# The last expert's first product before the other's second one, and half of the closing norm on the tensor engine

## The chip, the core and the metric

The kernel runs on one core of a Trainium2 chip. The core has a tensor engine (PE, whose weight loads the profile lists apart as PEld), a vector engine (DVE), a scalar engine (ACT), GpSimd (POOL) and SyncE (SP), which here issues nearly all transfers. Sixteen DMA engines move data between HBM and the on-chip memory (SBUF); PE writes its products to PSUM, eight banks of 128 partitions by 512 float32. The metric is the device time of one execution in microseconds (us).

## What is computed

One layer of a decoder trunk for 256 tokens of width 1024 in float32: a mixer, a norm, a mixture of experts, and a norm again. Only the last two matter here:

```python
def layer_norm(x, g, b):
    mu = jnp.mean(xf, axis=-1, keepdims=True)
    var = jnp.mean(jnp.square(xf - mu), axis=-1, keepdims=True)
    return ((xf - mu) * lax.rsqrt(var + LN_EPS) * g + b)
...
    def expert_block(args):
        h = xblk @ w1[e] + b1[e]                  # 1024 -> 2048
        gate, upv = jnp.split(h, 2, axis=-1)
        gate = jnp.minimum(gate, SWIGLU_LIMIT)
        upv = jnp.clip(upv, -SWIGLU_LIMIT, SWIGLU_LIMIT)
        act = (upv + 1.0) * (gate * jax.nn.sigmoid(SWIGLU_ALPHA * gate))
        return act @ w2[e] + b2[e]                # 1024 -> 1024
...
        h = moe_ffn(x, ...)                       # each token: 4 of 32 experts
        x = layer_norm(ALPHA * x + h, ln2_g[l], ln2_b[l])
```

An expert has 8 MB of w1 and 4 MB of w2; all 32 are read whole, 384 MB.

## The kernel before

The experts run one after the other, 0 to 31 (`E` is 32), each on up to 64 gathered tokens (a branch behind the end, not taken with these inputs, does the rest). Per expert:

- **First product** (`gemm1`, in `Last.first` for expert 31): the tokens stand still in PE 64 columns wide, w1 streams past; two halves (gate and up) fill the upper and lower 64 partitions of two PSUM banks, `h0` and `h1`. ACT and DVE copy the banks to `hs`.
- **Activation** (`act_steps`): PE transposes `hs` in two groups of four, DVE adds the bias, clips and multiplies, ACT takes the sigmoid. The result is `a`.
- **Second product** (`gemm2`, in `Last.second` for expert 31): `a` stands still, w2 streams past; ACT copies the bank to `ys`.
- **Scatter** (`scatter`): four products with the gate weights (`gT`) add `ys` to the four sums `acc[t][h]` (token tile t, column half h) that stay in PSUM.

The weights come in 2 MB loads (16 KB in a row for each partition) into a ring of 11 buffers: four loads for w1, two for w2. All are issued by SP in the order of the code (`in_order`, L1132). Up to expert 29 the order is w1 of expert e, then w2 of expert e-1, so that each second product stands behind the first product of the next expert and its activation is hidden. Behind that it is: w1 of 30, w2 of 30, w1 of 31, w2 of 31. The fourth load of w1 of 31 is cut into four pieces and the two loads of w2 of 31 into four by rows (`Last.load`, L1144). The code between L1358 and L1402 follows that order: second product of 30 (L1360), first product of 31 with the scatter of 30 between its rows, activation of 31 in two halves between the last products (L1371 to L1378), second product of 31. Its rows j 6 and 7 are split into two column halves of 256 (`columns`, L1392).

Calls through `PE`, `DVE` and `ACT` (class `Pinned`) keep the order of the code on their engine; calls through `nc.` may be placed by the scheduler.

The end: `add_sums` takes the moments of each 256 columns of `acc` on DVE (8 times `bn_stats`), `statistics` (L121) combines them and takes the square root on ACT, and `normed` (L1407) writes (x - mean) * rstd * g2 + b2 in four pieces of 128 tokens by 512 columns, each stored on its own. Three pieces are two DVE instructions each; the piece (0, 1) is one ACT instruction and two POOL instructions. `g2` and `b2` are the scale and the bias, spread over all partitions (`norm_rows`, some 110 us before the end).

## Time and profile before

| | |
|---|---|
| median of 3 runs | 1191.1 us (1190.51 to 1191.97) |
| the profiled execution | 1191.24 us |
| its span, first to last instruction | 1189.4 us |
| PE busy | 1126.8 us, 95% |
| DVE, ACT, POOL busy | 347.9, 208.8, 64.1 us |
| HBM traffic | 448 MB, 377 GB/s over the span |

The page of the profile gives busy time of each engine, the span in 40 equal slices, and the chain of waits that ended last. A time in a row is in us from the span's start; a float32 product shows as two matmul records, so that "x8" stands for four products. A bracket such as [0.69 <-ACT t L1212] is idle time of the engine just before the row and what ended it. A busy PE can be a PE that is also kept busy at just the pace of the loads.

### The profile page before, as it was taken

The page shows a single profiled execution, that of the slowest core. Times are in us where ns is not written, and L with a number is a line of the kernel's source. Part 1 is how long each engine was busy: PE and PEld are TensorE (multiplying, and loading weights), DVE is VectorE, ACT ScalarE, POOL GpSimd, SP SyncE. Part 2 cuts the span into 40 slices and gives each one's busy share as a digit, 9 for nine tenths or more (in the row PEclk, how much of TensorE's full clock was granted, in tenths as well). Part 3 has the DMA queues.
Part 4 walks back from the last instruction along what each step waited for, and adds up shares of the span by engine and source line. Part 5 has one row for each costly group of instructions (what it writes and reads, how often), then busy time and mean ns, then how long its engine had stood idle before and what let it go on. Part 6 is the DMA issues. An engine that isn't in the chain of part 4 may idle for free.

```text
span 1189.4 us, 15191 instructions
## 1 busy us (share of the span) xinstructions
PE 1126.8 (95%) x6440; PEld 594.2 (50%) x6441; DVE 347.9 (29%) x713; ACT 208.8 (18%) x494; POOL 64.1 (5%) x106
## 2 busy tenths in 40 slices
PE   9999999999999999999999898989898989899995
PEld 8998889985434343343434242424242424244432
DVE  6679776473111111111111111111111111111114
ACT  5115544432101010101101010101010101011101
POOL 1010001311000000000000000000000000000000
PEclk9999999999999999999999999999999999999998
DMA  8994329779999999999999999999999999999994
GB/s 246 321 298 142 107 75 377 301 272 370 422 430 430 428 430 427 428 429 429 428 428 431 429 430 429 428 428 430 429 429 430 428 429 429 428 429 430 428 417 182
DMA packets 72274, 449.33 MB, mean 378 GB/s; under 512 B 8084, under 2 KB 40778, under 8 KB 47498
## 3 DMA queue, kind: packets, MB, share of 16 engines
q1 hardware_dynamic: 71694, 447.50, 91.8%
q8 instruction: 52, 0.85, 0.3%
q10 hardware_dynamic: 508, 0.81, 0.2%
q14 instruction: 20, 0.16, 0.0%
HBM read 447.25 MB, written 1.05 MB: 377 GB/s over the span
## 4 chain that ended last, share of the span: by engine, by line
DMA 52%; PE 45%; DVE 2%; ACT 0%; issue 0%; SPq 0%; POOL 0%; POOLq 0%; DVEq 0%
DMA w<-in_moe_w_dram 50%; PE h L48 15%; PE u L48 8%; PE mm L94 4%; PE mm L95 4%; PE mm L96 4%; PE acc L48 2%; DMA w<-in_w_in_dram 1%; PE sc L648 1%; PE mm L48 1%; PE yps L693 1%; PE ptp L684 1%; PE sc L48 1%; PE ptp L48 0%; DVE t L48 0%; PE ptp L94 0%
## 5 line engine op out<-in xcount | busy, mean ns | idle before, releaser
L48 PE MATMUL h<-w,t 128*64 128x512 f32 x1448 | 320.1, 593 | 30.0 <-DMA w<-in_moe_w_dram 26.9
L48 PEld LDWEIGHTS h<-w,t 128*64 128x64 f32 x1448 | 101.9, 137 | 237.7 <-issue 181.8
L48 PE MATMUL u<-w,t 128*64 128x512 f32 x960 | 213.3, 596 | 1.5 <-DMA w<-in_moe_w_dram 1.3
L1107 DVE COPY t<-h 128x512 f32<-128x512 f32 x31 | 21.4, 692 | 507.2 <-PE h L48 507.2
L48 PE MATMUL h<-w,rws 128*64 128x512 f32 x640 | 141.6, 595 | 12.9 <-DMA w<-in_moe_w_dram 12.1
L48 PEld LDWEIGHTS u<-w,t 128*64 128x64 f32 x960 | 66.4, 137 | 125.5 <-issue 118.6
L48 PEld LDWEIGHTS h<-w,rws 128*64 128x64 f32 x640 | 44.8, 137 | 104.8 <-issue 81.6
L94 PE MATMUL mm<-xhl,ws 128*128 128x256 f32 x336 | 96.8, 288 | 0.0
L95 PE MATMUL mm<-xhl,ws 128*128 128x256 f32 x336 | 95.0, 283 | 0.0
L96 PE MATMUL mm<-xhl,ws 128*128 128x256 f32 x336 | 94.9, 283 | 0.0
L1106 ACT COPY t<-h 128x512 f32<-128x512 f32 x31 | 18.2, 586 | 434.4 <-PE h L48 434.4
L89 DVE TENSOR_TENSOR ws<-w,ws 128x1024 fp32r<-128x1024 f32 (+1 forms) x64 | 73.3, 1150 | 11.8 <-ACT ws L88 11.0
L1082 POOL TENSOR_TENSOR ext<-ext,G 128x128 f32<-128x128 f32 x62 | 27.1, 456 | 811.8 <-PE h L48 793.1
L48 PE MATMUL acc<-t,ext 64*128 64x512 f32 (+1 forms) x264 | 64.3, 603 | 0.9 <-ACT t L1212 0.7
L94 PEld LDWEIGHTS mm<-xhl,ws 128*128 128x128 f32 x336 | 64.3, 191 | 1.0 <-issue 0.8
L95 PEld LDWEIGHTS mm<-xhl,ws 128*128 128x128 f32 x336 | 64.4, 192 | 0.0
L96 PEld LDWEIGHTS mm<-xhl,ws 128*128 128x128 f32 x336 | 64.3, 191 | 0.0
L1199 DVE SCALAR_TENSOR_TENSOR t<-t 128x512 f32<-128x512 f32 x29 | 20.1, 692 | 150.1 <-PE u L48 150.0
L1212 ACT COPY t<-u 128x512 f32<-128x512 f32 x31 | 18.2, 586 | 177.4 <-PE u L48 177.4
L48 PEld LDWEIGHTS acc<-t,ext 64*128 64x128 f32 x264 | 23.2, 186 | 40.2 <-issue 28.5
L1195 ACT ACTIVATE t<-t 128x512 f32<-128x512 f32 (+2 forms) x36 | 20.7, 582 | 89.8 <-DVE t L1194 84.7
L88 DVE CAST ws<-w 128x1024 fp32r<-128x1024 f32 (+1 forms) x47 | 29.5, 636 | 24.0 <-PE mm L96 15.6
(340 smaller groups left out, 1095.3 us busy)
## 6 DMA issues: line engine op xcount, KB each, us to landing
w<-in_moe_w_dram SPq DMA_DIRECT2D x189, 2048.0 KB
w<-in_w_in_dram SPq DMA_DIRECT2D x22, 1024.0 KB
w<-in_w_up_dram SPq DMA_DIRECT2D x6, 1024.0 KB
w<-in_cmp_w_dram SPq DMA_DIRECT2D x4, 1024.0 KB
w<-in_w_o_dram SPq DMA_DIRECT2D x4, 1024.0 KB
w<-in_moe_w_dram SPq DMA_DIRECT2D x4, 1024.0 KB
w<-in_w_in_dram SPq DMA_DIRECT2D x6, 512.0 KB
w<-in_moe_w_dram SPq DMA_DIRECT2D x4, 512.0 KB
```

The lines of the kernel that those rows point to most:

```text
L48: return lambda *a, **k: self.tc.keep_in_program_order(f(*a, **k))
L88: copy(hi, src)
L89: return sub.tensor_tensor(lo, src, hi.bitcast(F32), op=OP.subtract).ins
L94: pe.matmul(p, ah, bh, start=first, stop=False, **kw)
L95: pe.matmul(p, ah, bl, start=False, stop=False, **kw)
L96: pe.matmul(p, al, bh, start=False, stop=last, **kw)
L1082: nc.gpsimd.tensor_tensor(SG[:, t], S[:, t, x:x + 1].to_broadcast([128, 2, SLOTS]), gsrc[:, t].unsqueeze(2).to_broadcast([128, 2, SLOTS]), ...
L1106: nc.scalar.copy(hs[:, :512], hp[0])
L1107: nc.vector.tensor_copy(hs[:, 512:], hp[1])
L1195: nc.scalar.activation(sg[i], gate[i], AF.Sigmoid, scale=1.702)
L1199: vec.scalar_tensor_tensor(a[:, js], up[i], 1.0, sg[i], op0=OP.add, op1=OP.mult)
L1212: nc.scalar.copy(ys, yp)
```

## The change

Three things are changed, all behind expert 30's activation:

1. **Order.** The loads become w1 of 30, w1 of 31, w2 of 30, w2 of 31. PE runs the whole first product of 31 (now by `gemm1`), the transposes of its activation, the second product of 30, the scatter of 30, and then the second product of 31. The activation of 31 writes to another buffer (`a_last`). Only the last load is cut: 1 MB by rows (j 4 and 5), then two pieces of 0.5 MB by columns, with 1 KB in a row.
2. **The end of the last product.** Column half 0 of rows 6 and 7, its copy, its four scatter products and its moments stand ahead of column half 1.
3. **The norm.** PE adds the bias `b2` through the identity into two free PSUM banks (`biased`, two products of 128x512, ahead of the second product of 31). For token tile 1 DVE makes only (x - mean) * g2, builds a diagonal matrix of rstd, and PE multiplies by it on top of the bias; ACT copies the bank out and issues the store. Token tile 0 is two DVE instructions for each half. POOL has no part in it any more.

```diff
     class Last:
         def load(self):
-            self.w1 = [new_rows(2) for _ in range(4)]
-            for q in range(3):
-                in_order(self.w1[q], w1v[E - 1, q])
-            for c in range(2):
-                for h in range(2):
-                    cs = slice(h * FF + c * 512, h * FF + (c + 1) * 512)
-                    in_order(self.w1[3][:, :, cs], w1v[E - 1, 3, :, :, cs])
             self.w2 = [new_rows(4) for _ in range(2)]
-            for q in range(2):
-                for r in (slice(0, 2), slice(2, 4)):
-                    in_order(self.w2[q][:, r], w2v[E - 1, q, :, r])
+            in_order(self.w2[0], w2v[E - 1, 0])
+            in_order(self.w2[1][:, :2], w2v[E - 1, 1, :, :2])
+            for c in range(2):
+                w, src = [v.rearrange("p r (h c) -> p r h c", h=2)[:, 2:, :, c * 256:(c + 1) * 256]
+                          for v in (self.w2[1], w2v[E - 1, 1])]
+                in_order(w, src)
             return self
...
+    def biased():
+        banks = [u_tile(), h_tile(1)]
+        for h, p in enumerate(banks):
+            PE.matmul(p, ident, b2[:, h * 512:(h + 1) * 512], start=True, stop=False, skip_group_check=True)
+        return banks
...
-            w2 = Second(e).load()
-            last = Last().load()
-            gemm2(a, w2)
...
-    banks = [h_tile(c) for c in range(2)]
-    for k in range(6):
-        for c in range(2):
-            last.first(banks, k, c)
-        if k == 1:
-            scatter(prev[1])
-    last.first(banks, 6, 0)
-    last.first(banks, 7, 0)
-    nc.scalar.copy(hs[:, :512], banks[0])
-    last.first(banks, 6, 1)
-    act(b1T[:, :, E - 1], a_main, 0, DVE, parts=2)
-    last.first(banks, 7, 1)
-    nc.scalar.copy(hs[:, 512:], banks[1])
-    act(b1T[:, :, E - 1], a_main, 1, DVE, parts=2)
+    w1, w2, last = First(E - 1).load(), Second(E - 2).load(), Last().load()
+    gemm1(xg[(E - 1) % 3], w1)
+    steps = [act_steps(b1T[:, :, E - 1], a_last, c, DVE, banks=[b]) for c, b in enumerate((u_tile(), h_tile(1)))]
+    for c in range(2):
+        next(steps[c])
+    gemm2(prev[0], w2)
+    for c in range(2):
+        for _ in steps[c]:
+            pass
+    scatter(prev[1])
+    banks = biased()
     yp = h_tile(0)
     for j in range(6):
         last.second(yp, j, slice(0, 512))
...
-    def normed(st):
+    def normed(st, banks):
         stats = [statistics(st[t]) for t in range(2)]
...
+        for c, p in zip(cols, acc[1]):
+            DVE.scalar_tensor_tensor(y[:, 1, c], p, stats[1][0], g2[:, c], op0=OP.subtract, op1=OP.mult)
+        DVE.reciprocal(stats[1][1], stats[1][1])
+        DVE.tensor_scalar(diag, ident, stats[1][1], None, op0=OP.mult)
+        DVE.reciprocal(stats[0][1], stats[0][1])
+        for c, p in zip(cols, banks):
+            PE.matmul(p, diag, y[:, 1, c], start=False, stop=True, skip_group_check=True)
+            ACT.copy(y[:, 1, c], p)
+            stores.append(nc.scalar.dma_start(ov[:, 1, c], y[:, 1, c]).ins)
+        for c, p in zip(cols, acc[0]):
+            d = y[:, 0, c]
+            DVE.scalar_tensor_tensor(d, p, stats[0][0], g2[:, c], op0=OP.subtract, op1=OP.mult)
+            DVE.scalar_tensor_tensor(d, d, stats[0][1], b2[:, c], op0=OP.mult, op1=OP.add)
+            stores.append(nc.sync.dma_start(ov[:, 0, c], d).ins)
```

How this moves instructions is shown at three places. First PE from the end of expert 31's first product to the split of its second one, before (`h_6716` and `h_6717` hold the first product of 31, `u<-ident` are transposes, `h_6788` is the second product of 31):

```order
L48 MATMUL h_6716<-w,t_3247 64x512 x4
L48 MATMUL h_6717<-w,t_3247 64x512 x2
L48 MATMUL u<-ident,t_3248 128x128 x4
L48 MATMUL h_6717<-w,t_3247 64x512 x2
L48 MATMUL u<-ident,t_3248 128x128 x4
L48 MATMUL h_6788<-w,t_3247 64x512 x12
L48 MATMUL h_6788<-w,t_3247 64x256 x8
```

and the same stretch in the changed kernel (`h_6696` is the first product's second bank, `u<-w` the second product of 30, the four `acc` its scatter, the `gb` rows the bias, `h_6779` the second product of 31):

```order
L48 MATMUL h_6696<-w,t_3247 64x512 x2
L48 MATMUL u<-ident,t_3248 128x128 x4
L48 MATMUL h_6732<-ident,t_3248 128x128 x4
L48 MATMUL u<-w,t_3247 64x512 x16
L48 MATMUL acc_3258<-t_3247,ext 128x512
L48 MATMUL acc_3259<-t_3247,ext 128x512
L48 MATMUL acc_3441<-t_3247,ext 128x512
L48 MATMUL acc_3442<-t_3247,ext 128x512
L48 MATMUL u<-gb_6428,ident 128x512
L48 MATMUL h_6776<-gb_6428,ident 128x512
L48 MATMUL h_6779<-w,rws 64x512 x12
L48 MATMUL h_6779<-w,rws 64x256 x4
```

Between the last first product and the last second product there now stand expert 30's second product, its scatter and the two bias products.

Second, the end of PE's list in the changed kernel, which before was the eight 64x256 products followed by eight `acc` products and nothing more:

```order
L48 MATMUL h_6779<-w,rws 64x256 x4
L48 MATMUL acc_3258<-t_3247,ext 128x256
L48 MATMUL acc_3259<-t_3247,ext 128x256
L48 MATMUL acc_3441<-t_3247,ext 128x256
L48 MATMUL acc_3442<-t_3247,ext 128x256
L48 MATMUL u<-t_3248,ext 128x512
L48 MATMUL h_6776<-t_3248,ext 128x512
```

Column half 1 now stands behind the scatter of half 0, and two products with the diagonal matrix (`ext`) close the list.

Third, DVE behind the moments, before:

```order
L48 BN_AGGR bn_mv<-st_6802 128x2
L48 SCALAR_TENSOR_TENSOR t_3248<-acc_3258,bn_mv,gb_6428 128x512
L48 RECIPROCAL rstd<-rstd 128x1 x2
L48 SCALAR_TENSOR_TENSOR nm<-bn_mv,rstd 128x1
L48 SCALAR_TENSOR_TENSOR t_3248<-t_3248,rstd,gb_6428 128x512
L48 SCALAR_TENSOR_TENSOR t_3248<-acc_3441,bn_mv,gb_6428 128x512
L48 SCALAR_TENSOR_TENSOR t_3248<-t_3248,rstd,gb_6428 128x512
L48 SCALAR_TENSOR_TENSOR t_3248<-acc_3442,bn_mv,gb_6428 128x512
L48 SCALAR_TENSOR_TENSOR t_3248<-t_3248,rstd,gb_6428 128x512
```

and in the changed kernel (`acc_3441` and `acc_3442` are token tile 1):

```order
L48 BN_AGGR bn_mv<-st_6793 128x2
L48 SCALAR_TENSOR_TENSOR t_3248<-acc_3441,bn_mv,gb_6428 128x512
L48 SCALAR_TENSOR_TENSOR t_3248<-acc_3442,bn_mv,gb_6428 128x512
L48 RECIPROCAL rstd<-rstd 128x1
L48 TENSOR_SCALAR ext<-ident,rstd 128x128
L48 RECIPROCAL rstd<-rstd 128x1
L48 SCALAR_TENSOR_TENSOR t_3248<-acc_3258,bn_mv,gb_6428 128x512
L48 SCALAR_TENSOR_TENSOR t_3248<-t_3248,rstd,gb_6428 128x512
L48 SCALAR_TENSOR_TENSOR t_3248<-acc_3259,bn_mv,gb_6428 128x512
L48 SCALAR_TENSOR_TENSOR t_3248<-t_3248,rstd,gb_6428 128x512
```

DVE has six instructions of 128x512 in both; the diagonal matrix comes behind the first two of them, and PE and ACT finish that tile.

## Rows read from the trace of the kernel before

**Rows 1.** The page: span, busy time of the engines, and what the transfers moved in each of 40 slices.

```profile
span 1189.4 us, 15191 instructions
PE 1126.8 (95%) x6440; PEld 594.2 (50%) x6441; DVE 347.9 (29%) x713; ACT 208.8 (18%) x494; POOL 64.1 (5%) x106
GB/s 246 321 298 142 107 75 377 301 272 370 422 430 430 428 430 427 428 429 429 428 428 431 429 430 429 428 428 430 429 429 430 428 429 429 428 429 430 428 417 182
```

**Rows 2.** The chain of waits that ended last, from 1115 us on: start, length, what.

```profile
1119.05 38.99 DMA w<-in_moe_w_dram
1158.06 15.11 DMA w<-in_moe_w_dram
1173.17 0.14 issue
1173.31 1.10 PE h L48 x8
...
1176.62 2.73 DVE st L1389 x8
...
1183.97 0.98 DVE t L48
```

**Rows 3.** Busy time by stretch at the end of the loads: stretch, its length, busy us and instructions of PE, PEld, DVE, ACT, POOL, granted clock of TensorE, busy share of the DMA engines, GB/s.

```profile
1164.00:1166.00 2.00, 2.00 (x11) 0.76 (x8) 0.73 (x2) 0.09 (x1) 0.00 (x0) 1.00 1.04 438
1170.00:1171.00 1.00, 1.00 (x8) 0.47 (x6) 0.66 (x3) 0.00 (x0) 0.00 (x0) 1.00 0.50 213
1172.50:1173.00 0.50, 0.50 (x4) 0.00 (x0) 0.00 (x0) 0.00 (x0) 0.00 (x0) 1.00 0.00 0
```

**Rows 4.** Instructions in order of time on PE, and one ACT copy: the fourth load of w1 of expert 30, the transposes behind it, the scatter behind those, the copy of the last expert's gate weights out of `h0`, the second product of 31 (two thirds of the row's records are its rows 0 to 5, the rest column half 0 of rows 6 and 7).

```profile
1133.69 3.65 PE L48 MATMUL h<-w,t 128*64 128x512 f32 x16 [1.13 <-DMA w<-in_moe_w_dram]
1137.55 1.40 PE L48 MATMUL u<-ident,t 128*128 128x128 f32 x8
1138.88 1.99 PE L48 MATMUL acc<-t,ext 64*128 64x512 f32 x8
1141.95 0.35 ACT L1095 COPY ext<-h 128x256 f32<-128x256 f32 x1
1167.80 6.59 PE L48 MATMUL h<-w,t 128*64 128x512 f32 x32 [0.16 <-PE u L48]
```

**Rows 5.** PE in expert 8's step, where a scatter stands right behind a second product and four products of 128x512 with the identity stand behind the scatter.

```profile
504.56 1.99 PE L48 MATMUL acc<-t,ext 64*128 64x512 f32 x8 [0.69 <-ACT t L1212]
506.47 3.70 PE L48 MATMUL acc<-x,ident_a 128*128 128x512 f32 x8
510.10 2.37 PE L48 MATMUL h<-w,t 128*64 128x512 f32 x10
```

**Rows 6.** Instructions in order of time between the last load and the norm, on ACT, PE and DVE.

```profile
1174.43 0.37 ACT L1396 COPY t<-h 128x256 f32<-128x256 f32 x1 [4.71 <-PE h L48]
1174.85 1.08 PE L48 MATMUL h<-w,t 128*64 128x256 f32 x8 [0.46 <-ACT t L1396]
1175.87 1.13 PE L48 MATMUL acc<-t,ext 64*128 64x256 f32 x8
1177.18 1.60 PE L48 MATMUL acc<-t,ext 64*128 64x256 f32 x8 [0.18 <-DVE st L1389]
1176.60 2.75 DVE L1389 BATCH_NORM_STATS2 st<-acc 128x6 f32<-128x256 f32 x8 [5.91 <-PE acc L48]
```

**Rows 7.** Instructions in order of time in the norm, on DVE and POOL.

```profile
1179.27 0.38 DVE L48 BATCH_NORM_AGGREGATE bn_mv<-st 128x2 f32<-128x24 f32 x2
1179.57 0.73 DVE L48 SCALAR_TENSOR_TENSOR t<-acc,bn_mv,gb 128x512 f32<-128x512 f32 x1
1180.22 0.21 DVE L48 RECIPROCAL rstd<-rstd 128x1 f32<-128x1 f32 x2
1180.48 0.75 DVE L48 SCALAR_TENSOR_TENSOR t<-t,rstd,gb 128x512 f32<-128x512 f32 x1
1181.14 0.75 DVE L48 SCALAR_TENSOR_TENSOR t<-acc,bn_mv,gb 128x512 f32<-128x512 f32 x1
1181.93 1.34 DVE L48 SCALAR_TENSOR_TENSOR t<-t,rstd,gb 128x512 f32<-128x512 f32 x1
1183.97 0.98 DVE L48 SCALAR_TENSOR_TENSOR t<-t,rstd,gb 128x512 f32<-128x512 f32 x1
1181.46 1.26 POOL L1418 TENSOR_TENSOR t<-t,gb 128x512 f32<-128x512 f32 x1 [67.93 <-ACT t L48]
1182.80 1.59 POOL L1419 TENSOR_TENSOR t<-t,gb 128x512 f32<-128x512 f32 x1
```

**Rows 8.** Busy time by stretch in the norm; columns as in Rows 3 (the granted clock is the third number from the end, 1.00 for 2.4 GHz and 0.50 for 1.2 GHz).

```profile
1178.60:1178.80 0.20, 0.18 (x1) 0.00 (x0) 0.20 (x2) 0.00 (x0) 0.00 (x0) 1.00 0.00 0
1180.80:1181.20 0.40, 0.00 (x0) 0.00 (x0) 0.40 (x2) 0.40 (x1) 0.00 (x0) 0.67 0.00 0
1181.20:1181.60 0.40, 0.00 (x0) 0.00 (x0) 0.40 (x2) 0.18 (x1) 0.14 (x1) 0.50 0.00 0
```

**Rows 9.** Transfers from 60 to 100 us, where nearly all packets are loads with 1 KB in a row: GB/s in 40 slices of 1 us, and the packets by size.

```profile
GB/s 349 347 362 336 349 346 205 45 88 342 385 358 354 346 348 355 349 357 347 348 348 347 347 361 382 389 135 37 0 6 72 375 414 385 364 347 135 0 0 0
DMA packets 9617, 10.76 MB, mean 269 GB/s; under 512 B 176, under 2 KB 8590, under 8 KB 9614
```

**Rows 10.** Transfers from 1180 to 1190 us, the four stores: GB/s in 40 slices of 0.25 us.

```profile
GB/s 0 0 0 0 0 0 0 0 156 410 401 82 0 0 0 0 172 393 410 74 0 295 393 393 352 418 213 49 25 82 8 0 0 0 0 0 0 0 0 0
```

More of the change, by code (lines that the diff above doesn't have):

```diff
@@ L1270, in overflow @@
                 add_sums(st, c)
-            normed(st)
+            normed(st, biased())
     def norm_rows():
@@ L1391, in hybrid @@
     st = row_sums()
-    columns = [slice(c * 256, (c + 1) * 256) for c in range(2)]
-    for cs in columns:
+    for c in range(2):
+        cs = slice(c * 256, (c + 1) * 256)
         for j in (6, 7):
@@ L1396, in hybrid @@
         nc.scalar.copy(ys[:, cs], yp[:, cs])
-    for c, cs in enumerate(columns):
         for t in range(2):
@@ L1405, in hybrid @@
     y = t1.rearrange("p (t d) -> p t d", t=2)
-    def normed(st):
+    def normed(st, banks):
         stats = [statistics(st[t]) for t in range(2)]
-        nm = lp.tile([128, 1], F32, name="nm")
-        def norm2(t, h, tail=None):
-            (mu, rs), c = stats[t], slice(h * 512, (h + 1) * 512)
-            d = y[:, t, c]
-            out_q = nc.sync
-            if tail is None:
-                out_q = nc.scalar
-                ACT.activation(d, acc[t][h], AF.Identity, bias=nm, scale=rs)
-                nc.gpsimd.tensor_tensor(d, d, g2[:, c], op=OP.mult)
-                nc.gpsimd.tensor_tensor(d, d, b2[:, c], op=OP.add)
-            else:
-                DVE.scalar_tensor_tensor(d, acc[t][h], mu, g2[:, c], op0=OP.subtract, op1=OP.mult)
-                tail()
-                DVE.scalar_tensor_tensor(d, d, rs, b2[:, c], op0=OP.mult, op1=OP.add)
-            return out_q.dma_start(ov[:, t, c], d).ins
-        def scales():
-            for _, rs in stats:
-                DVE.reciprocal(rs, rs)
-            DVE.scalar_tensor_tensor(nm, stats[0][0], -1.0, stats[0][1], op0=OP.mult, op1=OP.mult)
-        return [norm2(0, 0, scales), norm2(0, 1)] + [norm2(1, h, lambda: None) for h in range(2)]
@@ L1433, in hybrid @@
-    overflow(normed(st))
+        diag = ext[:, 512:640]
+        cols = [slice(h * 512, (h + 1) * 512) for h in range(2)]
+        stores = []
+        for c, p in zip(cols, acc[1]):
[7 more added lines that the diff above has]
+            stores.append(nc.scalar.dma_start(ov[:, 1, c], y[:, 1, c]).ins)
```

12 lines of the change are left out of this document (5 added, 7 removed).

## The prediction

> **What bounds the kernel now.** I read the page first: PE is busy 95% of the span, yet the transfers run at 428 to 431 GB/s in slice after slice [rows 1], so one of the two only follows the other. The chain of waits tells which: it jumps from load to load, 38.99 us for eight of them, 4.87 us for 2 MB, down to 1173.17 us [rows 2]. PE needs 3.65 us for a load (16 records) and waits 1.13 us for it [rows 4]. So as long as loads come, their count sets the time, and this change moves the same 384 MB. Only what lies behind the last load is to be won: 1173.31 us to the end of the span, 16.1 us, and the start of that stretch can be lost.
>
> Is PE free when the last load lands? The transfers thin out to 213 GB/s by 1170 us (a busy share of 0.50: half of the DMA engines are done, the others go on at their pace) and are over by 1172.5 us; PE is busy for the whole of both stretches there, to 1173.0 us [rows 3]. Rows 0 to 5 of the last product take from 1167.80 us to 1173.31 us, where column half 0 begins [rows 2, 4]. So PE and the last load meet within 0.2 us. **There is no spare time on PE in front of 1173.3 us**; whatever the new order puts in there shows.
>
> **The order of PE and loads.** Counting loads from 1133.69 us, when the fourth load of w1 of 30 is there [rows 4], at 4.87 us each [rows 2]: in the new order w1 of 31 is complete four loads later, at 1153.2 us; the two loads of w2 of 30 land at 1158.05 and 1162.9 us, the first of w2 of 31 at 1167.8 us, and the last pieces as before at about 1173.2 us, since the bytes are the same. The ring does not stall them: its 11 buffers are handed out in the same sequence, and the last load takes the buffer of the first load of w1 of 30, which PE has left before 1133.69 us [rows 4].
>
> PE then goes like this. The first product of 31 begins later than its load, because it writes `h0`, which the copy of the last gate weights leaves at 1142.3 us [rows 4]; that costs nothing, its loads arrive until 1153.2 us. From there to the end of the transposes expert 30 took 5.19 us (1133.69 to 1138.88) [rows 4]: 1158.4 us. The first half of expert 30's second product is done 3.6 us later, at 1162.0 us, the load of the second half lands at 1162.9 us and is done by 1166.55 us. Behind that everything is PE alone:
>
> - The scatter of 30 now stands directly behind its second product, so PE waits for ACT to copy the bank: 0.69 us, then 1.91 us for the scatter (504.56 to 506.47) [rows 5]. Before, the scatter stood two loads into the next product, where the copy was long done.
> - The bias: two products of 128x512 with the identity. Four of the same shape took 506.47 to 510.10 us, 3.63 us [rows 5], so two take 1.8 us. These are new work on PE; nothing hides them.
> - Rows 0 to 5 of the second product of 31: 5.4 us (1167.80 to 1173.17) [rows 2, 4].
>
> Sum: 1166.55 + 0.69 + 1.91 + 1.8 + 5.4 = 1176.35 us, against 1173.31 us: **+3.0 us**. The activation of 31, which before stood between the last products, is free now, covered by the second product of 30; but before it was covered too, by the last loads. All pieces of w2 of 31 are long there: with 1 KB in a row loads run at about 350 GB/s [rows 9] instead of 430, which makes 1 MB 0.6 us later, against 3 us of cover.
>
> **Column halves.** Before, from column half 0 on: product 1.12 us, copy, half 1 from +1.54 us (it waits for the copy), scatter of half 0 at +2.56, moments from +3.29 for 2.75 us, so +6.04 us [rows 2, 6]. Now the scatter of half 0 takes the place at +1.54, its moments run from +2.27 to +3.65 us (four of eight), half 1 comes at +2.5, its copy ends at +4.0, scatter, moments from +4.75 to +6.1 us, from the same steps [rows 6]. The moments of half 0 now lie under the product of half 1, but half 1 comes a scatter later, and the two cancel: **+0.1 us**.
>
> **The norm.** Before, from the combining of the moments at 1179.27 to the end of the last DVE piece at 1184.95 us: 5.68 us [rows 2, 7]. In it, DVE instructions of 128x512 follow each other at 0.65 us alone (1179.57 to 1180.22, 1180.48 to 1181.14), but the ones that read both operands from SBUF while POOL works take 1.34 and 0.98 us [rows 7]. Now six at 0.65 us without POOL, 0.3 us ahead of the first, and some 0.35 us for two reciprocals (0.1 us each) and the diagonal matrix (a quarter of the 0.65 us at least): 0.3 + 6 x 0.65 + 0.35 + 0.1 = 4.65 us, a gain of 1.0 us on the DVE side. The four stores of 256 KB then come within 1.4 us of each other and queue: each needs about 0.7 us at 400 GB/s [rows 10], which gives back some 0.1 us. So at best **-0.9 us**.
>
> The other side is PE. The diagonal matrix is ready 1.9 us behind the start of the combining (0.3 + 1.3 + 0.3). At full clock the products take 0.9 us each [rows 5], ACT's copies 0.6 us, and the second store of tile 1 is issued before DVE's last one: no loss. But before, the granted clock stood at 1.00 to 1180.8 us and at 0.50 from 1181.2 us; the last product had ended at 1178.78 us (1177.18 + 1.60) [rows 6, 8]. The pause was 2.2 us. In the new tail PE has nothing to do from the last scatter, 0.6 us ahead of the end of the moments (1 us if the moments no longer pace it) until the diagonal matrix: 2.4 to 2.8 us, a little longer than what the clock outlasted. At 1.2 GHz each product takes 1.8 us, the second copy ends 6.4 us behind the start of the combining, and ACT's last store is issued 0.7 us later than the last one before: **+0.6 us**. The bounds are thus -0.9 and +0.6 us; one fall in one profile says that it comes about then, not on which side of the first product, so I take the middle, **-0.2 us**, and keep both ends.
>
> The Trainium skill's page "TensorE: Matmul & The Clock Gate" (section "What's actually happening") says that the throttled clock is the default and that activity releases it, which speaks against putting two products behind a pause. By that rule alone both run at 1.2 GHz and the sum would be +3.7 us; no row here shows a product behind such a pause.
>
> **Sum.** 3.0 + 0.1 - 0.2 = +2.9 us. The profiled execution took 1191.24 us, 1.84 us more than its span [rows 1]; it lies 0.14 us above the median of 1191.1 us. So 1191.1 + 2.9 = **1194.0 us**. About 0.2% (2.4 us) is what a measurement of this kernel can tell from no change: below 1188.7 is faster, above 1193.5 slower.
>
> **Rivals.**
> - *The clock holds.* Both diagonal products run at 2.4 GHz, the norm gains its whole 0.9 us: 1191.1 + 3.0 + 0.1 - 0.9 = 1193.3 us, within 0.2%. For it: the pause is only some tenths longer than the one that the clock outlasted. It decides if the first product starts less than about 2.2 us behind the last scatter.
> - *The clock falls first.* +3.7 us, 1194.8 us.
> - *Not slower: the last load still sets the tail.* If PE reaches column half 0 before its piece lands, at about 1172 us, then only half 1 is left behind 1173.2 us: product 1.1, copy 0.4, scatter 0.7 and half of the moments 1.4 us, 1176.8 us instead of 1179.35 us, and with the norm's 0.9 us the time is 1187.7 us, faster. It decides where PE's work behind 1162.9 us is under 9.2 us. Against it: my rows give 13.4 us, and to save 4 us neither the scatter nor the bias may cost anything.
> - *A load holds PE.* If the cut pieces were so slow that half 1 waits for them (from 1178.9 us on), the time goes above 1195 us. Against it stand 5 us of cover.
>
> **How the numbers follow.** Forecast (clock falls between) 0.42, clock holds 0.25, clock falls first 0.22, last load sets the tail 0.07, load holds PE or another mishap 0.04. Each of the first three has some 0.6 us of its own spread (the waits of 0.7 us, the medians). Slower: of the forecast 0.30, of the clock that holds 0.08, of the clock that falls first 0.20, of the mishaps 0.03: 0.61. Faster: the last load's 0.07. Same: the rest, 0.32. The range from 1191.9 to 1195.6 us takes in the bounds of the norm with their spread and leaves out the last two cases and a little at each end.
>
> **What would show it.** Right: in the trace of the changed kernel PE waits about 0.7 us in front of the scatter of 30 for ACT's copy, two identity products of 0.9 us follow, column half 0 begins at about 1176.3 us with no wait for a load in front of it, moments end at about 1182.4 us, and DVE's six instructions stay near 0.65 us apart. The granted clock at the two diagonal products separates the first two rivals. Wrong: PE waiting for a load at rows 6 and 7, or column half 0 before 1175 us; or a norm that takes over 6.3 us to its last store.

## The result: slower, by more than forecast

| | changed | before, same chip |
|---|---|---|
| median | 1198.94 us (1197.82 to 1199.77, 6 runs) | 1191.52 us (1190.51 to 1192.38, 6 runs) |
| ratio | 1.0062, 95% interval 1.0053 to 1.0072 | |
| profiled execution | 1198.55 us, span 1196.8 us | 1191.24 us, span 1189.4 us |

The change costs 7.4 us, where 2.9 us were forecast and the range ended at 1195.6 us. The direction was right; the size was not.

The page of the changed kernel: span, busy time of PE, and what the transfers moved in 40 slices.

```profile
span 1196.8 us, 15192 instructions
PE 1131.9 (95%) x6448; PEld 594.7 (50%) x6449; DVE 347.3 (29%) x706; ACT 208.5 (17%) x492; POOL 61.3 (5%) x104
GB/s 245 326 288 142 106 85 387 287 287 359 427 427 428 428 427 427 427 428 427 428 427 426 428 427 428 427 428 428 427 428 428 427 427 427 427 428 429 428 425 112
```

Against [rows 1], the slices in the long middle read 427 to 428 GB/s more often than 428 to 430. This is 0.3%, and easily read past. PE is busy for 5.1 us more in all.

The chain of waits of the changed kernel, from 1087 us on: start, length, what.

```profile
1087.79 39.09 DMA w<-in_moe_w_dram
1126.94 39.33 DMA w<-in_moe_w_dram
1166.31 3.68 PE u L48 x16
1170.65 1.99 PE acc L48 x8
1173.69 7.05 PE h L48 x34
1188.29 2.08 PE u L48 x2
```

The loads hand over to PE at 1166.31 us, the second half of the second product of 30, as the prediction had it (it said 1162.9 us). The two links between loads are 39.1 and 39.3 us long, where [rows 2] have 38.99 us.

PE of the changed kernel in order of time, from the fourth load of w1 of 30 on: start, length, engine, line, what, idle time before it and what ended that. The bias is `u<-gb,ident` and `h<-gb,ident`; the row x32 is rows 0 to 5 of the last product (24 records, three quarters of it, not the two thirds that [rows 4] has for the same row of before) and column half 0 of rows 6 and 7 (8 records).

```profile
1136.70 3.65 PE L48 MATMUL h<-w,t 128*64 128x512 f32 x16 [1.15 <-DMA w<-in_moe_w_dram]
...
1166.31 3.65 PE L48 MATMUL u<-w,t 128*64 128x512 f32 x16 [1.00 <-DMA w<-in_moe_w_dram]
1170.65 1.99 PE L48 MATMUL acc<-t,ext 64*128 64x512 f32 x8 [0.69 <-ACT t L1202]
1172.57 1.12 PE L48 MATMUL u<-gb,ident 128*128 128x512 f32 x2
1173.53 1.02 PE L48 MATMUL h<-gb,ident 128*128 128x512 f32 x2
1174.48 6.23 PE L48 MATMUL h<-w,rws 128*64 128x512 f32 x32
1181.24 1.13 PE L48 MATMUL acc<-t,ext 64*128 64x256 f32 x8 [0.53 <-ACT t L1387]
1182.31 1.08 PE L48 MATMUL h<-w,rws 128*64 128x256 f32 x8
1183.86 1.13 PE L48 MATMUL acc<-t,ext 64*128 64x256 f32 x8 [0.47 <-ACT t L1387]
1188.29 2.08 PE L48 MATMUL u<-t,ext 128*128 128x512 f32 x2 [3.29 <-DVE ext L48]
1190.15 1.57 PE L48 MATMUL h<-t,ext 128*128 128x512 f32 x2
```

The first row is the finding. It stands ahead of everything that the change reorders, and it begins 3.0 us later than the same row of before (1133.69 us [rows 4]). The delay grows while the experts run: the first expert's first product begins no later than before. The chain of waits has it as the row below, first of before and then of the changed kernel.

```profile
276.23 13.88 PE h L48 x64
```

```profile
276.05 13.88 PE h L48 x64
```

The rest of the tail is what was drawn: the wait of 0.69 us and the scatter, the bias for 1.91 us, no load in the way of the last product.

DVE and ACT of the changed kernel in the norm, and below it the stretches there (columns as in [rows 3]; the granted clock is the third number from the end).

```profile
1184.60 1.43 DVE L1380 BATCH_NORM_STATS2 st<-acc 128x6 f32<-128x256 f32 x4 [1.19 <-PE acc L48]
1185.94 0.38 DVE L48 BATCH_NORM_AGGREGATE bn_mv<-st 128x2 f32<-128x24 f32 x2
1187.94 0.29 DVE L48 TENSOR_SCALAR ext<-ident,rstd 128x128 f32<-128x128 f32 x1
1191.76 0.59 ACT L48 COPY t<-h 128x512 f32<-128x512 f32 x1 [0.78 <-PE h L48]
```

```profile
1186.00:1187.00 1.00, 0.00 (x0) 0.00 (x0) 0.96 (x4) 0.48 (x2) 0.00 (x0) 1.00 0.00 0
1187.00:1188.00 1.00, 0.00 (x0) 0.00 (x0) 0.89 (x4) 0.00 (x0) 0.00 (x0) 0.92 0.00 0
1188.00:1188.40 0.40, 0.11 (x1) 0.12 (x1) 0.40 (x3) 0.00 (x0) 0.00 (x0) 0.50 0.00 0
1188.40:1190.00 1.60, 1.60 (x2) 0.72 (x3) 1.56 (x3) 0.00 (x0) 0.00 (x0) 0.50 0.05 10
```

PE has nothing to do from 1184.99 us on, until the first diagonal product at 1188.29 us. The granted clock still is 1.00 (2.4 GHz) in 1186 to 1187 us, and 0.50 (1.2 GHz) around the start of that product: 2.08 us for the two records that took 1.12 us as bias. The last copy ends at 1192.35 us, 6.41 us behind the start of the combining, where before it was 5.68 us [rows 7].

Where the 7.4 us between the two spans are, each stretch measured from row to row:

| stretch | before | changed | difference | forecast |
|---|---|---|---|---|
| start of the span to the fourth load of w1 of 30 | 1133.69 | 1136.70 | +3.0 | 0 |
| from there to column half 0 (1173.31; 1179.63, which is the end of the row x32 less 1.08 us for its last 8 records) | 39.62 | 42.93 | +3.3 | +3.0 |
| column half 0 to the end of the moments (1179.35; 1186.03) | 6.04 | 6.40 | +0.4 | +0.1 |
| moments to the last DVE or ACT instruction's end (from 1179.27; from 1185.94) | 5.68 | 6.41 | +0.7 | -0.2 |
| from there to the end of the span | 4.45 | 4.45 | 0.0 | 0 |

One thing in the diff that the prediction passed over has to do with the first line of the table. With the old `normed` goes its tile `nm`, one float32 for each partition, from the pool `late`. It takes 32 bytes per partition in the memory plan of the built program (the places that the program's buffers get in SBUF), and `late` lies at the right end of SBUF, so the pools to its left move up by 32 bytes, weight buffers among them. The start of each of the eleven 16 KB buffers, as bytes behind a multiple of 256:

| kernel | `ring_x`, `ring_c` (3 buffers) | `ring_a` (4) | `ring_b`, `ring_d` (4) | on a multiple |
|---|---|---|---|---|
| before | 0 | 128 | 64 | 3 of 11 |
| changed | 32 | 128 | 64 | 0 of 11 |

### The profile page after: what moved, and what is told of

Read it like the earlier page. It is cut to its first block, busy times and chain, and to the rows that moved or that the text cites. A ratio compares the mean times of both kernels' runs of the same rounds, so it can differ in the third digit from the quotient of the medians.

```text
span 1196.8 us, 15192 instructions
## 1 busy us (share of the span) xinstructions
PE 1131.9 (95%) x6448; PEld 594.7 (50%) x6449; DVE 347.3 (29%) x706; ACT 208.5 (17%) x492; POOL 61.3 (5%) x104
## 4 chain that ended last, share of the span: by engine, by line
DMA 54%; PE 44%; DVE 1%; ACT 1%; issue 0%; SPq 0%; DVEq 0%; ACTq 0%
DMA w<-in_moe_w_dram 52%; PE h L48 14%; PE u L48 8%; PE mm L94 4%; PE mm L95 4%; PE mm L96 4%; PE acc L48 2%; DMA w<-in_w_in_dram 1%; PE sc L648 1%; PE mm L48 1%; PE yps L693 1%; PE ptp L684 1%; PE sc L48 1%; PE ptp L48 0%; DMA x<-in_x_dram 0%; PE ptp L94 0%
## 5 line engine op out<-in xcount | busy, mean ns | idle before, releaser
L48 PE MATMUL h<-w,t 128*64 128x512 f32 x1408 | 312.5, 595 | 33.1 <-DMA w<-in_moe_w_dram 28.8
L48 PEld LDWEIGHTS h<-w,t 128*64 128x64 f32 x1408 | 98.9, 137 | 236.8 <-issue 176.7
L48 PE MATMUL h<-w,rws 128*64 128x512 f32 (+1 forms) x680 | 149.0, 590 | 13.4 <-DMA w<-in_moe_w_dram 12.6
L48 PEld LDWEIGHTS h<-w,rws 128*64 128x64 f32 x680 | 47.6, 137 | 110.1 <-issue 84.8
L1185 ACT ACTIVATE t<-t 128x512 f32<-128x512 f32 (+1 forms) x34 | 20.6, 605 | 91.8 <-DVE t L1184 84.7
```

The source lines that it names most:

```text
L48: return lambda *a, **k: self.tc.keep_in_program_order(f(*a, **k))
L1185: nc.scalar.activation(sg[i], gate[i], AF.Sigmoid, scale=1.702)
```

## The experiments

**Theory A**: the shift by 32 bytes slows every load a little, and that is the +3.0 us; the change itself costs about 4 us in the tail. **Rival B**: the new order, or something else in the change, slows the loads. Times below are medians; ratios are to the runs of before on the same chip, with 95% intervals.

**1. The changed kernel with its 32 bytes back.** The reciprocal goes to a tile of its own again.

```diff
+        nm = lp.tile([128, 1], F32, name="nm")
...
-        DVE.reciprocal(stats[1][1], stats[1][1])
-        DVE.tensor_scalar(diag, ident, stats[1][1], None, op0=OP.mult)
+        DVE.reciprocal(nm, stats[1][1])
+        DVE.tensor_scalar(diag, ident, nm, None, op0=OP.mult)
```

> The changed kernel, but with a tile of 128x1 (32 bytes for each partition) in the pool 'late' again, which the change had dropped; rstd of token tile 1 goes through it, nothing else differs. With it the three weight buffers of the right side start at 203520, 154368 and 170752 bytes again instead of 32 bytes higher. Theory A (where the buffers start sets the rate of the loads): 3.0 us less than the changed kernel, 1195.9 us, 16 KB packets at 614 ns instead of 616. Theory B (the loads are slower for another reason, the new order or the new program): no difference, 1198.9 us.

Measured: 1195.4 us, ratio 1.0035 (1.0022 to 1.0049); 3.5 us less than the changed kernel. The fourth load of w1 of 30 in this run, and the last product up to the end of column half 0:

```profile
1133.48 3.65 PE L48 MATMUL h<-w,t 128*64 128x512 f32 x16 [1.15 <-DMA w<-in_moe_w_dram]
...
1170.90 6.24 PE L48 MATMUL h<-w,rws 128*64 128x512 f32 x32
```

The load is back where before had it (1133.69 us [rows 4]).

**2. The kernel before with 32 bytes less.** `nm` is written into a column that is no longer read.

```diff
-        nm = lp.tile([128, 1], F32, name="nm")
+        nm = mvs[-1][:, 1:2]
```

> The kernel before, with its tile of 128x1 dropped (its value goes into a column that is no longer read), so that the three buffers of the right side start 32 bytes higher as in the changed kernel; same instructions, same order. Theory A: 3.0 us slower than before, 1194.5 us, 16 KB packets at 616 ns. Theory B: no difference, 1191.5 us.

Measured: 1194.81 us, ratio 1.0027 (1.0016 to 1.0038), and with no instruction reordered the same row is late:

```profile
1136.86 3.65 PE L48 MATMUL h<-w,t 128*64 128x512 f32 x16 [1.15 <-DMA w<-in_moe_w_dram]
```

Theory A holds in both directions; rival B falls.

**3. The order alone.** Order, loads and column halves of the changed kernel, the norm and the buffers of before.

```diff
-    banks = biased()
...
-    def normed(st, banks):
+    def normed(st):
...
-    overflow(normed(st, banks))
+    overflow(normed(st))
```

> The order, the loads and the column halves of the changed kernel with the norm of before (no bias products, no diagonal products); buffers start where they did before. Theory A: column half 0 begins 1.4 us later than before (3.35 us in the changed kernel less the 1.9 us of the two bias products), the halves cost 0.3 us, the norm nothing: 1193.3 us. Theory B with the order of the loads as the cause: 3 us more, 1196.3 us.

Measured: 1192.66 us, ratio 1.0011 (1.0002 to 1.002), +1.5 us on the 1191.12 us of before. The prediction's terms for this part are 3.0 - 1.8 (the bias) + 0.1 = 1.3 us.

**4. The norm alone.** Order and loads of before, and the new norm with its bias ahead of the second product of 31.

```diff
+    nbanks = biased()
     yp = h_tile(0)
...
-    overflow(normed(st))
+    overflow(normed(st, nbanks))
```

> The order, the loads and the halves of before with the norm of the changed kernel, its bias products directly ahead of the second product of 31; buffers start where they did before. Theory A: 1.9 us for the bias products, which nothing hides, and 0.7 us for the norm with diagonal products at the lower clock: 1194.1 us. Theory B with the new program as the cause: 1197 us.

Measured: 1194.06 us, ratio 1.0026 (1.0015 to 1.0038), +2.9 us. Its terms in the table above are 1.9 (bias) + 0.7 = 2.6 us. So the two parts cost 1.5 and 2.9 us apart, and 4.3 us together in run 1 (1195.4 against 1191.12): they add up.

**5. The bias later.** Run 1 with the bias behind the last scatter, where PE waits for the norm.

```diff
-    banks = biased()
     yp = h_tile(0)
...
+    banks = biased()
     ov = out[0].rearrange("(t p) d -> p t d", p=128)
```

> The kernel of e1, but with the two bias products behind the last scatter instead of ahead of the second product of 31: there PE waits more than 3 us for the diagonal matrix. Theory A (the bias products cost their 1.9 us on PE because nothing hides them, and the pause lets the clock fall): both go, 1.9 us from the start of column half 0 and 1.3 us from the diagonal products, which now run at 2.4 GHz: 1192.2 us. Rival C (PE's place is not what counts, the tail waits for something else): no difference to e1, 1195.4 us.

Measured: 1193.23 us, ratio 1.0011 (1.0002 to 1.002), 2.2 us less than run 1, where theory A asked for 3.2 us. The bias off the path is 1.9 us of that. It also fills the pause, and the diagonal products then take 1.13 and 1.02 us, as the bias did; but of the 1.3 us that theory A put on them next to nothing reaches the end (run 8):

```profile
1182.80 1.13 PE L48 MATMUL u<-t,ext 128*128 128x512 f32 x2 [1.37 <-DVE ext L48]
1183.77 1.02 PE L48 MATMUL h<-t,ext 128*128 128x512 f32 x2
```

**6. All eleven buffers on multiples of 256 bytes.** The kernel before, with 128 bytes in front of `ring_a` and 64 among the constants, nothing else.

```diff
+    ctx.enter_context(tc.tile_pool(name="gap", bufs=1, side="left")).tile([128, 32], F32, name="gap")
     ring_a = ctx.enter_context(tc.tile_pool(name="ring_a", bufs=NA, side="left"))
...
+    consts.tile([128, 16], F32, name="gap2")
     ident = consts.tile([128, 128], F32, name="ident")
```

> The kernel before with 128 and 64 bytes of unused space ahead of the left buffers, so that all eleven weight buffers start on a multiple of 256 bytes (before: three do, four start 128 and four 64 bytes behind one); nothing else differs. Theory A1 (it is the multiple of 256 that counts): 3 us for three buffers make some 8 us for eight, 1183 us, packets below 614 ns. Theory A2 (it is the multiple of 64, which all have before): no difference, 1191.1 us.

Measured: 1186.39 us, ratio 0.9951 (0.9938 to 0.9965): faster than both kernels, by 5.0 us against before, though not by the 8 us of theory A1. Its transfers, in 40 slices:

```profile
GB/s 254 329 285 143 107 79 373 303 276 368 425 432 429 430 431 430 430 431 430 429 432 431 430 430 430 430 432 432 429 431 430 429 432 431 430 430 432 429 425 182
```

The middle runs at 429 to 432 GB/s. Part of the gain is earlier: the experts' row below begins at 274.99 us, and at 276.23 us in before, so 1.2 us are won in the mixer, whose loads use the buffers of `ring_a` too. The traces differ in this row: from 273.6 to 275.0 us in the four runs with `ring_a` moved (6, 9, 11, 12), from 275.4 to 276.7 us in all others. The table behind run 14 therefore counts from it.

```profile
274.99 13.88 PE h L48 x64
```

**7. The three good buffers moved by 64 bytes.** The kernel before with 64 bytes more in `late`; `ring_x` and `ring_c` then start 192 bytes behind a multiple of 256, and are still on one of 64.

```diff
+    lp.tile([128, 16], F32, name="gap3")
     xp = ctx.enter_context(tc.tile_pool(name="ring_x", bufs=1, side="right", reuse_waits="tile"))
```

> The kernel before with 64 bytes of unused space, so that the three buffers of the right side start 64 bytes lower: on a multiple of 64, no longer of 256. Theory A1: as e2, 3 us slower, 1194.3 us, packets at 616 ns. Theory A2: no difference, 1191.1 us, packets at 614 ns.

Measured: 1194.2 us, ratio 1.0024 (1.0015 to 1.0033). So to be on a multiple of 64 is not enough. That 128 is not enough either, and 256 is, run 10 shows.

**8. The clock held.** Run 1 with three more products of the bias shape behind the last scatter, into a bank that nobody reads. They are throwaway work that keeps PE busy in the pause.

```diff
+    idle = h_tile(0)
+    for i in range(3):
+        PE.matmul(idle, ident, b2[:, :512], start=True, stop=True, skip_group_check=True)
```

> The kernel of e1 with three products of 128x512 of the identity with the bias behind the last scatter; they go into a bank that nobody reads, and add work that the result does not need. Theory A: the granted clock stays at 1.00 through the diagonal products, which take 0.95 us each instead of 2.0 and 1.4, 1.3 us less than e1: 1194.1 us. Rival: the clock falls anyway, or the throwaway products delay the diagonal ones: 1195.4 us or more.

Measured: 1195.38 us, ratio 1.0029 (1.0017 to 1.004), the time of run 1. Yet the clock did hold. PE and ACT at the end, and below them a stretch:

```profile
1185.14 1.12 PE L48 MATMUL u<-t,ext 128*128 128x512 f32 x2 [0.51 <-DVE ext L48]
1186.10 1.02 PE L48 MATMUL h<-t,ext 128*128 128x512 f32 x2
...
1187.39 0.58 ACT L48 COPY t<-h 128x512 f32<-128x512 f32 x1 [0.51 <-DVE t L48]
```

```profile
1186.00:1187.00 1.00, 1.00 (x3) 0.19 (x1) 1.00 (x2) 0.58 (x1) 0.00 (x0) 1.00 0.07 16
```

From the combining (1182.80 us) to the last instruction's end (DVE, 1188.04 us) the norm takes 5.24 us, against 6.46 us in run 1 (1182.35 to 1188.81). But from there to the end of the span it is 5.8 us here and 4.1 us in run 1. All traces of the three kinds of norm say the same:

| norm | combining to the last instruction's end, us | from there to the end of the span, us | together, us |
|---|---|---|---|
| old: before, runs 3, 6 | 5.68, 5.67, 5.66 | 4.45, 4.16, 4.77 | 10.1, 9.8, 10.4 |
| new, clock at 0.50: changed, runs 1, 4, 9 | 6.41, 6.46, 6.74, 6.76 | 4.45, 4.09, 4.75, 4.52 | 10.9, 10.6, 11.5, 11.3 |
| new, clock at 1.00: runs 5, 8, 11 | 5.24, 5.24, 5.24 | 5.30, 5.76, 5.66 | 10.5, 11.0, 10.9 |

What the faster products win, 1.2 to 1.5 us, is nearly all lost again behind the last instruction. In runs 1 and 8 the first store is issued some 3.9 us behind the combining (1186.21 and 1186.66 us), and 1 MB in four stores follows. That the stores' transfer takes the place of the slow clock is what these rows suggest; it was not tried with smaller stores. That the fall of the clock is worth little here is shown: some 0.2 us between the means of the last two lines, less than what the traces of one line differ by.

**9. The changed kernel on multiples of 256.** The two gaps of run 6 in the kernel of run 1.

```diff
+    ctx.enter_context(tc.tile_pool(name="gap", bufs=1, side="left")).tile([128, 32], F32, name="gap")
...
+    consts.tile([128, 16], F32, name="gap2")
```

> The changed kernel with its 32 bytes back (1195.4 us) and all eleven weight buffers on multiples of 256 bytes. Theory A (the place of the buffers sets the rate of the loads, and what the change itself does to the tail is a separate cost of about 4 us): the 5.0 us that the same places took off the kernel before come off here too, 1190.4 us, and the distance to the kernel before on the same places (1186.4) stays at 4 us. Rival (the change moves the loads' own pace by its order): the faster loads meet the changed order's waits, and less than half of the 5 us comes, 1193 us or more.

Measured: 1190.29 us, ratio 0.9988 (0.9979 to 0.9997). It is 5.1 us under run 1 and 3.9 us above run 6. The two effects add, and its fourth load of w1 of 30 is there when that of run 6 is (1128.85 us in both); the changed order has no part in the pace of the loads.

**10. Only loads.** 384 loads of 2 MB into eleven buffers in turn, a copy of one column behind each, nothing else computed and zeros stored. The starts change every 48 loads: a multiple of 256, then 32, 64 and 128 bytes behind one, and the same once more.

```python
for start in STARTS:
    for i in range(48):
        room = ring.tile([128, 4096 + 64], F32, name="w")
        w = room[:, start // 4:start // 4 + 4096]
        tc.keep_in_program_order(nc.sync.dma_start(w, src[n % len(src)]))
        nc.vector.tensor_copy(y[:, n % 1024:n % 1024 + 1], w[:, 4095:4096])
        n += 1
```

> Only the loads: all expert weights in the order of the kernel, 16 KB for each partition into eleven buffers in turn, a copy of one column behind each, nothing else computed and zeros stored. The buffers start, for 48 loads at a time and twice over, on a multiple of 256 bytes, then 32, 64 and 128 bytes behind one. Theory A1 (the start of the target relative to 256 bytes sets the pace of a load, whatever else runs): 48 loads take 0.5 to 0.9% longer (1.2 to 2.1 us of about 233) in the stretches at 32, 64 and 128 bytes than in those at 256, both times. Rival (the pace suffers where PE reads a neighbouring buffer while one is written, and the start by itself is nothing): all eight stretches within 0.2% of each other.

Stretches from the copy behind a group's first load to the copy behind its last, 47 loads each (stretch, length, DVE, POOL, clock, busy share of the DMA engines, GB/s); the first two are the first turn at 256 and at 32, the last two the second turn at 256 and at 32:

```profile
8.82:237.60 228.78, 7.23 (x47) 0.00 (x0) 1.00 1.01 431
242.49:472.94 230.45, 7.24 (x48) 0.00 (x0) 1.00 1.01 428
...
948.84:1177.82 228.98, 7.24 (x47) 0.00 (x0) 1.00 1.01 431
1182.72:1413.18 230.46, 7.24 (x48) 0.00 (x0) 1.00 1.01 428
```

The groups at 64 and at 128 take 230.46 to 230.86 us. So a start off the multiple costs 0.65 to 0.9%, both times, with PE idle: it is the load itself, not a clash with PE's reads, and not another of the tiles that a gap moves in the kernel.

The Trainium skill's page "DMA: Bandwidth & Descriptors" (section "How a descriptor splits into AXI transactions") says that a transaction must start at an address that is a multiple of 256 bytes, and that the first one of a descriptor which starts off one begins at the boundary below. An estimate from that is 65 transactions in place of 64 for 16 KB, 1.6%. The page speaks of the bytes that are fetched, not of where a load's target starts. The direction agrees with runs 6, 7 and 10; the 0.65 to 0.9% of run 10 are about half of it.

**11. The new norm with a late bias, on multiples of 256.** Order and loads of before, the norm of run 5, the gaps of run 6. Against run 4:

```diff
+    ctx.enter_context(tc.tile_pool(name="gap", bufs=1, side="left")).tile([128, 32], F32, name="gap")
...
+    consts.tile([128, 16], F32, name="gap2")
...
-    nbanks = biased()
     yp = h_tile(0)
...
+    nbanks = biased()
     ov = out[0].rearrange("(t p) d -> p t d", p=128)
```

> The order and the loads of the kernel before, the new norm of the second token tile with its bias behind the last scatter, and all buffers on multiples of 256 bytes. Theory (the new norm saves some 0.5 us up to the issue of the last store where the clock holds or PE pauses under 1.5 us, as the run with the bias late showed): 1185.9 us against 1186.4 of the kernel before on these places. Rival (the four stores then stand closer and their transfer ends the program, as the run with the clock held showed, which brought the last store 0.9 us forward and the end by nothing): 1186.4 to 1187.2 us.

Measured: 1186.51 us, ratio 0.9953 (0.994 to 0.9967), against 1186.39 us of run 6. The medians can't tell theory and rival apart: they lie 0.6 us apart, and the five runs of each kernel spread over 1.7 to 1.9 us. The traces speak for the rival: from the combining to the end of the span it is 10.9 us here and 10.4 us in run 6, so no gain from the new norm is seen even with its bias off the path.

**12. Only `ring_a` moved.** The kernel before with the first gap alone; `ring_a` is on multiples of 256, `ring_b` and `ring_d` are 192 bytes behind one.

```diff
+    ctx.enter_context(tc.tile_pool(name="gap", bufs=1, side="left")).tile([128, 32], F32, name="gap")
```

> The kernel before with only the four buffers of ring_a moved from 128 bytes behind a multiple of 256 onto one; the four of ring_b and ring_d stay off it. Theory A1 (each buffer counts by itself, and 128 bytes off costs as 64 does): half of the 5.0 us, 1188.7 us. Rival (only starts off a multiple of 128 bytes cost anything, so that ring_b and ring_d held all of the 5 us): 1191.4 us, no change.

Measured: 1186.22 us, ratio 0.9957 (0.9943 to 0.997): the whole 5 us, with 4 of 11 buffers still off. Not all of it comes from the experts' loads: the experts begin 2.4 us earlier than in before, and the fourth load of w1 of 30 is there 5.6 us earlier.

```profile
273.81 13.88 PE h L48 x64
1128.10 3.65 PE L48 MATMUL h<-w,t 128*64 128x512 f32 x16 [1.14 <-DMA w<-in_moe_w_dram]
```

So 3.2 us are won between these two rows, where run 6 wins 3.6 us. Theory A1, by which each buffer pays for its own start, would have half of 3.6 us; it falls. Theory A3 takes its place: a start counts by how many of the other buffers, taken in turn, are on a multiple.

**13. Patterns of starts, only loads.** As run 10, with the pattern of a kernel for 44 loads at a time and each twice. A pattern has the start of each of the eleven buffers in the order in which the kernel takes them.

```diff
-        for start in STARTS:
-            for i in range(48):
+        for pattern in PATTERNS:
+            for i in range(44):
+                start = (128 + int(pattern.split()[i % 11])) % 256
```

> Loads alone as in the run of the loads alone, with eleven buffers in the order in which the kernel takes them (b b a x a d d c c a a), 44 loads for each pattern of starts behind a multiple of 256 bytes, all patterns twice over. Patterns: all 0; all 192; all 64; before (b, d 64, a 128, x, c 0); changed (as before, x and c 32); the kernel before shifted by 64 bytes (x and c 192); ring_a moved (b, d 192, the rest 0); b and d at 64, the rest 0. Zeros stored, nothing else computed. Theory A1 (each load pays for its own start): all 0 at 4.87 us a load, all off at 4.905, before between with 8 of 11 (4.895), ring_a moved at 4.883 with 4 of 11, the same with b and d at 64. Theory A3 (a start counts by what the loads around it have, as the run with ring_a moved has it): ring_a moved is as fast as all 0, 4.87, while before is at 4.89 and the patterns with no buffer on a multiple are at 4.905.

Stretches from the fifth load of a group to its last, 39 loads each; columns as in run 10. The rows are all on a multiple, before, changed, `ring_a` moved, and the same four in the second turn.

```profile
28.10:218.07 189.97, 5.99 (x40) 0.00 (x0) 1.00 1.01 431
...
673.41:864.60 191.19, 6.00 (x40) 0.00 (x0) 1.00 1.01 430
889.10:1080.08 190.98, 6.00 (x40) 0.00 (x0) 1.00 1.01 428
...
1320.26:1510.55 190.29, 6.00 (x40) 0.00 (x0) 1.00 1.01 431
...
1749.47:1938.98 189.51, 6.00 (x40) 0.00 (x0) 1.00 1.01 431
...
2395.59:2585.86 190.27, 6.00 (x39) 0.00 (x0) 1.00 1.01 430
2610.33:2802.02 191.69, 5.99 (x39) 0.00 (x0) 1.00 1.01 428
...
3042.46:3232.00 189.54, 5.99 (x39) 0.00 (x0) 1.00 1.01 431
```

| pattern | on a multiple | us for 39 loads, first and second turn | us a load, mean |
|---|---|---|---|
| all 0 | 11 of 11 | 189.97, 189.51 | 4.865 |
| `ring_a` moved | 7 | 190.29, 189.54 | 4.870 |
| `ring_b`, `ring_d` at 64, the rest 0 | 7 | 189.58, 190.26 | 4.870 |
| before | 3 | 191.19, 190.27 | 4.890 |
| changed | 0 | 190.98, 191.69 | 4.906 |
| run 7 | 0 | 191.38, 191.61 | 4.910 |
| all 64 | 0 | 191.04, 190.88 | 4.896 |
| all 192 | 0 | 190.98, 191.67 | 4.906 |

The two turns of a pattern differ by up to 0.9 us, as much as some neighbours in the table do. But the GB/s column sorts the groups without an overlap: 431 with seven or eleven on a multiple, 430 with three, 428 to 429 with none (one last stretch reads 415 because the loads end in it). With some 190 loads in the program, an estimate from the means is 190 x 0.016 = 3.0 us between changed and before, and 190 x 0.025 = 4.8 us between before and all on a multiple; the kernels showed 3.0 to 3.7 and 5.0 us, of which 1.2 us were won in the mixer.

**14. Only `ring_b` and `ring_d` moved.** The kernel before with 192 bytes among the constants; `ring_a` stays 128 bytes off.

```diff
+    consts.tile([128, 48], F32, name="gap2")
```

> The kernel before with only the four buffers of ring_b and ring_d moved onto multiples of 256 bytes; ring_a stays 128 bytes behind one. Theory A1: half of the 5.0 us, 1188.9 us. Theory A3 (a few buffers off do nothing when the others are on): 1186.4 us. Third: the 128 bytes of ring_a are the whole cost and moving the others brings nothing, 1191.5 us.

Measured: 1187.25 us, ratio 0.9969 (0.9958 to 0.998), 4.0 us under before: nearer to A3 than to half of the 5 us. The 1 us to run 6 is about the size of what run 6 won in the mixer. In run 14 the experts begin as late as in before, and the fourth load of w1 of 30 is there 2.9 us earlier:

```profile
276.27 13.88 PE h L48 x64
1130.80 3.65 PE L48 MATMUL h<-w,t 128*64 128x512 f32 x16 [1.15 <-DMA w<-in_moe_w_dram]
```

The kernels side by side, the times within the kernel from one trace each; the fourth column is the time from the experts' first row to the fourth load of w1 of 30, and leaves the mixer out:

| kernel | on a multiple | fourth load of w1 of 30 at, us | from the experts' first row, us | median, us |
|---|---|---|---|---|
| 2: before, 32 bytes off | 0 of 11 | 1136.86 | 860.75 | 1194.81 |
| 7: before, 64 bytes off | 0 | 1136.05 | 860.03 | 1194.2 |
| before | 3 | 1133.69 | 857.46 | 1191.5 |
| 14: `ring_b`, `ring_d` moved | 7 | 1130.80 | 854.53 | 1187.25 |
| 12: `ring_a` moved | 7 | 1128.10 | 854.29 | 1186.22 |
| 6: all moved | 11 | 1128.85 | 853.86 | 1186.39 |
| changed | 0 | 1136.70 | 860.65 | 1198.94 |
| 1: changed, 32 bytes back | 3 | 1133.48 | 857.40 | 1195.4 |
| 9: changed, all moved | 11 | 1128.85 | 854.10 | 1190.29 |

The fourth column goes by the count alone, in both orders of the work: 860.0 to 860.8 us with none on a multiple, 857.4 to 857.5 with three, 854.3 to 854.5 with seven, 853.9 to 854.1 with all.

## Why the prediction was wrong, step by step

- **What bounds the kernel**: right that the loads do. Up to 1166 us they set the time, and everything that was lost in the tail showed at the end. That their count alone sets it ("this change moves the same 384 MB") is the assumption that the next point is about.
- **"The last pieces as before at about 1173.2 us, since the bytes are the same"**: this is the step that failed. The bytes were the same, but not the addresses that they went to. The prediction took 4.87 us for a load out of the trace as if it belonged to the load's size; it belonged to the places of the ring's buffers too, and the diff moved three of these by dropping a tile of 4 bytes at the other end of the program. Runs 1 and 2 show it: 3.5 us back with the 32 bytes, 3.7 us lost without them. Of the 4.9 us between forecast and result this is 3.0 us; the rest is 0.3 us, 0.3 us and 0.9 us in the three terms below and 0.4 us in the median of before. With the 32 bytes back the change takes 1195.4 us, inside the range and near its upper end.
- **PE alone behind the last load of w2 of 30, +3.0 us**: right. The wait of 0.69 us is there, the bias takes 1.91 us (1.8 forecast), no load stands in the way of the last product, and the stretch measured +3.3 us. Most of the 0.3 us over is the slower loads again: the second half of expert 30's second product begins 29.61 us behind the fourth load, 29.2 forecast. In run 1, with the buffers back, the row x32 begins at 1170.90 us, and the stretch from 1133.48 us to column half 0 (1176.06 us) is 42.58 us, +2.96 us. Run 3 gives +1.5 us for the order without the bias; 1.3 us follow from the terms.
- **Column halves, +0.1 us**: +0.4 us. The steps come in the order drawn, but the lag grows from 0.1 us at the scatter of half 0 to 0.3 us at the end: PE waits 0.53 and 0.47 us for ACT's copies, and the last moments take 1.43 us instead of 1.35.
- **The norm, between -0.9 and +0.6 us, taken -0.2 us**: mis-sized. It measured +0.7 us, just past the upper bound. The case behind that bound came true nearly to the letter (the second copy ends 6.41 us behind the start of the combining, 6.4 forecast); what failed is the middle taken between two cases. The pause was 3.29 us, not 2.4 to 2.8: the diagonal matrix was ready 2.29 us behind the start of the combining (1185.94 to 1188.23 us), not 1.9, and PE's last scatter had ended 0.95 us ahead of it. In 1188.0 to 1188.4 us, where the first product begins, the clock was at 0.50. The rule from the Trainium skill that the prediction set aside ("TensorE: Matmul & The Clock Gate", section "What's actually happening") agrees with the trace: both products began at 0.50.
- **The bound below, -0.9 us**: did not come even with the clock held. In runs 5, 8 and 11 the norm takes 5.24 us to its last instruction's end, where 4.65 were forecast; against the old norm that wins 0.4 us, but the end of the span stands 1.1 us further behind it (5.6 us in the mean, 4.5 with the old norm), so that the new norm loses 0.7 us even then. The term of 0.1 us for the queue of the four stores was too small; how much of it is the stores' own pace stays open.
- **The rivals**: "the clock falls first" (1194.8 us) is what happened in the tail, and with the buffers in their old places (run 1) it is 0.6 us off. "The last load still sets the tail" and "a load holds PE" did not come about. The rival that did most, a slower pace of all loads, was not among them.
- **What stays open**: why 4 buffers of 11 off a multiple cost only some 0.5 us when the other 7 are on one (runs 12 to 14), and why a start of 32 bytes costs nearly as much as one of 128 (230.5 against 230.7 to 230.8 us in run 10). The times follow the count of buffers on a multiple; the same count in another arrangement was tried for seven alone, and no run shows the mechanism.

## What to carry to other kernels

Before taking the pace of the loads out of an old trace, compare the memory plans of the two programs: a small tile added or dropped in a pool moves the pools behind it on its side of SBUF, and in a kernel that is bound by loads for hundreds of microseconds, a shift by 32 bytes cost 3.5 us, nearly as much as everything that the change did to the tail (4.3 us). Put the buffers of a weight ring on multiples of 256 bytes; two gaps of 128 and 64 bytes per partition won 5.0 us here. Where a step ends in several stores within two microseconds, measure to the end of the program: here a gain of 1.2 us ahead of the last stores did not reach it.

## What the runs showed of the hardware

- A load of 2 MB with 16 KB in a row took 4.865 us with all eleven buffers on multiples of 256 bytes and 4.90 to 4.91 us with none, with nothing else running (run 13).
- With 7 of 11 on a multiple the pace was that of all 11, to within what two turns differ by (4.870 us, run 13); in the kernel it cost 0.2 to 0.7 us over some 854 us (runs 12 and 14 against 6 and 9).
- In the changed kernel the granted clock was still 1.00 in the stretch that ended 2.0 us behind PE's last work, and 0.50 in the one that began 3.0 us behind it; the next product ran at 0.50.
